# x loaded in pairs of tiles ahead of its small tables, and two products of each Strassen pair moved one pair ahead

## The chip, the cores and the metric

The kernel runs on one core of a Trainium2 chip. The time is the device time of one execution in microseconds (us); lower is better. The core has TensorE (PE, matmuls, writing to PSUM banks), VectorE (DVE), ScalarE (ACT), GpSimd (POOL) and SyncE (SP). Each engine works through its own instructions in order. Here SP issues nearly all loads, and POOL those that add onto what is already in SBUF.

## The reference

A trunk of two layers over a sequence of 512 tokens of width 1024, all in float32.

```
x: (1, 512, 1024)
layer 0:  h = rmsnorm(x);  z = h @ w_in
          a = gelu(u) * spatial_gating(gelu(v))          # 4 groups, 128 x 128 position mixing
          b = latent attention(q rank 384, kv rank 256, 32 rotary columns, 8 heads)
          x = x + concat(a, b) @ w_out
          x = x + swiglu(rmsnorm(x))                      # width 2816
layer 1:  x = x + retention(rmsnorm(x))                   # 4 heads, gated
          x = x + swiglu(rmsnorm(x))
swiglu(h) = (silu(h @ w_gate) * (h @ w_up)) @ w_down
```

## The kernel before

Activations lie transposed: x is eight tiles of 128 features by 512 tokens. Every product in full precision is made of three matmuls on halves of the numbers (`hi`, and `lo`, the rest), so each weight chunk of up to 128 x 1024 is loaded to `w_raw`, cast by ACT to `w_hi` (L214) and subtracted by DVE to `w_lo` (L215).

The weights come in one order, the tape. `tape_spec` lists the chunks, `Tape.load` makes the next one, `tape.ahead()` keeps four chunks made ahead of use (four buffers of `w_hi` and `w_lo`). `w_raw` has three buffers in the mixers and seven in the FFNs. All chunk loads go to SP's queue (L211).

**Head (L427 to L457).** x tile 0 is issued on SP, then the first chunk in four pieces, then x tiles 1 to 7. Each x tile is scaled by a gain (`scaled_parts`: `h_hi` on ACT, L356, and `h_lo` on DVE, L357), and its squares are summed for the norm (ACT L309, DVE L310). Five small tables (2 to 128 KB, 354 KB with a broadcast one of 96 KB) are issued on POOL's queue: `cgain`, `wk`, `qkg`, `rope0`, `vgain`. The first PE work is five projections of 24 matmuls with these chunks; then come the rotary key (`wk`, whose tile is scaled on DVE in L490), the attention and the gating.

**FFN (`ffn`).** Gate and up for 22 tiles of 128 columns. The first two column tiles ("whole") are done plainly. The others are done in ten pairs p = 1 to 10 by a Strassen-like scheme: seven products a pair, called A11, A12, A22 (weights as loaded, or "load"), S1, S3 (two weight blocks summed by an accumulating POOL load, L213, "sum") and S2, S4 (a block added to an earlier raw chunk by DVE, L199, "add": S2 is made from the raw chunks of A11 and S1, S4 from those of A12 and S2, so these `w_raw` buffers are held until then). A product is 24 matmuls of 256 columns (L865). It uses sums of activations, `t_hi` and `t_lo`, that ACT and DVE make at the start of the FFN (`sums`, L835 to L847, L281, L282).

PSUM banks: `xs` (`ps_x`) holds A11, onto which S2, S3 and A22 are added in turn; `vs` (`ps_v`) holds S1 and then S4; `ws` (`ps_w`) holds A12. Between these, ACT copies what is needed from `xs` to the wide tiles `rows` (`take`, L894) and DVE adds the others (`add`, L897); the next product into `xs` must wait for that copy. `finish` (L877 to L883) makes the activated result of a tile, and after the pairs 3, 7 and 10 the down projection runs over what is done so far (`down`).

The order of the products is written by hand in `ffn_steps`, for the tape and for the compute loop alike. The program is then laid out by a planner that walks it by priority in program order with its own estimates of durations, and may put a later instruction ahead of one that it takes to be not ready.

Of the kernel before, what the change touches and what calls it, by code (L numbers as in the profile page):

```python
# [10 lines left out]
F32 = mybir.dt.float32  # L11
# [5 lines left out]
P = 128  # L17
D = 1024
S = 512
KD = D // P  # L20
# [12 lines left out]
PAIRS = MF // 2  # L33
# [5 lines left out]
def ffn_steps():  # L39


    steps = [("whole", 0)]
    for p0, p1 in FF_PARTS:
        for p in range(max(p0, 1), p1):
            if p == 1:
                steps.append(("A11", p))
            steps += [("S1", p), ("S2", p), ("A12", p), ("S3", p)]
            if p + 1 < PAIRS:
                steps.append(("A11", p + 1))
            steps += [("A22", p), ("S4", p)]  # L50
        steps.append(("down", (p0, p1)))
    return steps

# [101 lines left out]
def turns(m, d):  # L155


    if m.shape[1] == 2 * d:
        return m.rearrange("p (j d) -> p d j", j=2)
    return m.rearrange("p (b j d) -> p b d j", j=2, d=d)  # L160
# [75 lines left out]
def trunk_kernel(ctx: ExitStack, tc: tile.TileContext, a: dict, out: bass.AP):  # L236
    nc = tc.nc
    const = ctx.enter_context(tc.tile_pool(name="const", bufs=1))
    parts = ctx.enter_context(tc.tile_pool(name="parts", bufs=Tape.DEPTH))
    res = ctx.enter_context(tc.tile_pool(name="res", bufs=1))  # L240
# [12 lines left out]
    def bank(name="bank"):  # L253
        return ps.tile([P, S], F32, name=name, tag="bank")

    tape = Tape(nc, parts, a["wtape"])
# [3 lines left out]

    gains = const.tile([P, 4, KD], F32, name="gains")
    nc.scalar.dma_start(out=gains, in_=a["gains"])
    x = [res.tile([P, S], F32, name=f"x{k}") for k in range(KD)]
    ident = const.tile([P, P], F32, name="ident")
    make_identity(nc, ident)
    ones = const.tile([P, P], F32, name="ones")
# [10 lines left out]
    def f32(t):  # L277
        return t.bitcast(F32)
# [66 lines left out]
    def h_tiles(k):  # L345
        return (
            hres.tile([P, S], F32R, name=f"h_hi{k}"),
            hres.tile([P, S], F32R, name=f"h_lo{k}"),
        )

    def scaled_parts(which, k):


        hi, lo = h_tiles(k)
        g = gains[:, which, k : k + 1]
        nc.scalar.activation(hi, x[k], AF.Identity, scale=g)  # L356
        nc.vector.scalar_tensor_tensor(  # L357
            lo, x[k], g, f32(hi), op0=ALU.mult, op1=ALU.subtract
        )
        return hi, lo  # L360

    def project(h, n=1, name="ps_mm", d=HALF):

        w = [tape.next() for _ in range(n)]
        accs = [bank(name) for _ in range(n)]
        nk = w[0][0].shape[1]
        for k in range(nk):
            for (hi, lo), acc in zip(w, accs):
                mm3(acc, (hi[:, k, :], lo[:, k, :]), h[k], k == 0, k == nk - 1, d)
        tape.ahead()  # L370
        return accs[0] if n == 1 else accs
# [55 lines left out]
    with ExitStack() as e:  # L427
        new_raw(e, 3)
        h = []
        for k in range(KD):  # L430
            nc.sync.dma_start(out=x[k], in_=a["xT"][k * P : (k + 1) * P, :])
            if k == 0:
                tape.load(pieces=4)
            h.append(scaled_parts(0, k))
        tape.load(pieces=2)
        tape.ahead()
        new_tmp(e)
# [5 lines left out]
        for k in range(KD):  # L443
            ss.add(x[k])

        vgain = ev.tile([P, 4], F32, name="vgain")
        cgain = ev.tile([P, 5], F32, name="cgain")
        qkg = ev.tile([P, 2, QK0], F32, name="qkg")
        rope0 = ea.tile([P, NT, 2, ROPE], F32, name="rope0")
        nc.gpsimd.dma_start(out=cgain, in_=a["lat_gT"])  # L450
        wk = ea.tile([P, KD, ROPE], F32, name="wk")
        nc.gpsimd.dma_start(out=wk, in_=a["kpe_w"])
        nc.gpsimd.dma_start(
            out=qkg, in_=a["qk_g"].rearrange("(o j) f -> o j f", o=1).broadcast_to([P, 2, QK0])
        )
        nc.gpsimd.dma_start(out=rope0, in_=a["rope0"])
        nc.gpsimd.dma_start(out=vgain, in_=a["gm_gT"])  # L457


        lat, latp = [], []  # L460
# [151 lines left out]
        w = [tape.next() for _ in range(3)]  # L612
# [37 lines left out]
        def u_tile():  # L650
# [13 lines left out]
            out=bs, in_=a["gm_b"].rearrange("(o g) t -> o g t", o=1).broadcast_to([P, 4, P])  # L664
# [147 lines left out]
    def ffn(h, ss, which):  # L812
# [7 lines left out]
        with ExitStack() as e:  # L820
# [7 lines left out]
            def wide():  # L828
                return fp2.tile([P, 2 * S], F32, name="J", bufs=4)
# [26 lines left out]
            def products(acc, name, start):  # L856

                hi, lo = tape.next()
                for k in range(KD // 2):
                    mh, ml = (turns(v, q // 2) for v in stands[name][k])  # L860
                    for f in range(2):
                        o = acc[:, f * q : (f + 1) * q]
                        cols = slice(f * P, (f + 1) * P)
                        for n, (s, m) in enumerate(((hi, mh), (hi, ml), (lo, mh))):
                            nc.tensor.matmul(  # L865
                                o,
                                s[:, k, cols],
                                m,
                                start=start and k + f + n == 0,
                                stop=k == KD // 2 - 1 and n == 2,  # L870
                                skip_group_check=True,
                            )

            def finish(m, g, u, own):

                t = fp2.tile([P, S], F32, name="t")
                nc.vector.tensor_tensor(own(t), g, own(R), op=ALU.mult)  # L877
                nc.scalar.activation(t, t, AF.Silu)
                nc.vector.tensor_tensor(own(t), own(t), u, op=ALU.mult)  # L879
                hi = fp.tile([P, S], F32R, name=f"a_hi{m % 8}")  # L880
                lo = fp.tile([P, S], F32R, name=f"a_lo{m % 8}")
                split(hi, lo, t)
                act[m] = (hi, lo)  # L883

            def in_psum(acc):
                return acc.rearrange("p (f d j) -> p f j d", f=2, j=2)

            def side(t, i):

                t = t.rearrange("p (f t) -> p f t", f=2)[:, :, i * q : (i + 1) * q]  # L890
                return t.rearrange("p f (j d) -> p f j d", j=2)

            def take(t, i, acc, sign=1.0):
                nc.scalar.activation(side(t, i), in_psum(acc), AF.Identity, scale=sign)  # L894

            def add(t, i, acc, op=ALU.add):
                nc.vector.tensor_tensor(side(t, i), side(t, i), in_psum(acc), op=op)  # L897
# [29 lines left out]
            whole = [project(h, 2)]  # L927
# [6 lines left out]
            own = lambda t: t  # L934
            for name, p in ffn_steps():
                if name == "A11":
                    xs, rows = bank("ps_x"), [wide(), None]
                    products(xs, name, True)
                    take(rows[0], 0, xs)
                    following = (xs, rows)  # L940
                    if p == 1:
                        R = ss.rows(norm)
                        for m in range(2):
                            finish(m, undone(whole[m][0]), undone(whole[m][1]), plain)
                if name == "S1":
                    xs, rows = following
                    vs = bank("ps_v")
                    products(vs, name, True)
                if name == "S2":
                    products(xs, name, False)  # L950
                    take(rows[0], 1, xs)
                if name == "A12":
                    ws = bank("ps_w")
                    products(ws, name, True)
                    add(rows[0], 0, ws)
                if name == "S3":
                    products(xs, name, False)
                    rows[1] = wide()
                    take(rows[1], 1, xs, -1.0)
                    add(rows[1], 1, vs, ALU.subtract)  # L960
                    here = (xs, rows)
                if name == "A22":
                    xs, rows = here
                    products(xs, name, False)
                    take(rows[1], 0, xs, -1.0)
                    finish(2 * p + 1, rows[1][:, :S], rows[1][:, S:], own)
                if name == "S4":
                    products(vs, name, False)
                    add(rows[0], 1, vs)
                    finish(2 * p, rows[0][:, :S], rows[0][:, S:], own)  # L970
                if name == "down":
                    last = p[1] == PAIRS
                    for m in down(*p):
                        if last:
                            yield m
                elif name != "whole":
                    tape.ahead()

    h = [scaled_parts(2, k) for k in range(KD)]
# [6 lines left out]
    h, ss = h2, ss2  # L986


    with ExitStack() as e:
# [9 lines left out]
        def parts_tile(name, n=S):  # L999
            return (od.tile([P, n], F32R, name=name + "_hi"), od.tile([P, n], F32R, name=name + "_lo"))  # L1000
# [20 lines left out]
        for hd in range(RH):  # L1021
# [17 lines left out]
            k = rotated("k", accs2)  # L1039
# [21 lines left out]
            for j in range(NT - 1):  # L1061
                n = S - j * P
# [15 lines left out]
                p = parts_tile(f"att{j}", n)  # L1078
# [117 lines left out]
```

## Time and profile before

| | |
|---|---|
| median of 3 runs | 1240.56 us (1240.27 to 1242.06) |
| profiled execution | 1239.42 us, its span 1237.6 us |
| mean granted TensorE clock | 0.997 |
| PE busy | 1219.7 us, 99% of the span |
| DVE busy | 853.4 us, 69% |
| ACT busy | 563.0 us, 45% |
| DMA | 155.32 MB, mean 125 GB/s |

The span runs from the first to the last instruction. PE's matmuls are pipelined and their ends are modelled, so its busy share says that it hardly waits, not that it is at its peak. Other engines' idle time costs nothing unless PE waits for them.

### The profile page before, as it was taken

The page shows a single profiled execution, that of the slowest core. Times are in us where ns is not written, and L with a number is a line of the kernel's source. Part 1 is how long each engine was busy: PE and PEld are TensorE (multiplying, and loading weights), DVE is VectorE, ACT ScalarE, POOL GpSimd, SP SyncE. Part 2 cuts the span into 40 slices and gives each one's busy share as a digit, 9 for nine tenths or more (in the row PEclk, how much of TensorE's full clock was granted, in tenths as well). Part 3 has the DMA queues.
Part 4 walks back from the last instruction along what each step waited for, and adds up shares of the span by engine and source line. Part 5 has one row for each costly group of instructions (what it writes and reads, how often), then busy time and mean ns, then how long its engine had stood idle before and what let it go on. Part 6 is the DMA issues. An engine that isn't in the chain of part 4 may idle for free. (4 is left out here: it accounts for less than half of the span.)

```text
span 1237.6 us, 18425 instructions
## 1 busy us (share of the span) xinstructions
PE 1219.7 (99%) x7464; PEld 1106.2 (89%) x7464; DVE 853.4 (69%) x1226; ACT 563.0 (45%) x811; POOL 85.5 (7%) x89
## 2 busy tenths in 40 slices
PE   8999999999999999999999999999998999999998
PEld 6897778898999899888888888888888989998997
DVE  6597748986597577955474574574778756875774
ACT  5465746653366245534242242242466524652551
POOL 2062000100000000000000000000010000000000
PEclk9999999999999999999999999999999999999999
DMA  7223115655575556132231332332265565754631
GB/s 233 83 75 120 35 34 171 168 173 153 139 193 172 144 144 177 72 119 102 69 102 68 103 102 69 102 103 68 86 180 161 171 151 139 204 162 128 166 108 68
DMA packets 44980, 155.32 MB, mean 125 GB/s; under 512 B 5232, under 2 KB 5776, under 8 KB 44768
## 3 DMA queue, kind: packets, MB, share of 16 engines
q1 hardware_dynamic: 38304, 130.70, 31.7%
q0 software_dynamic: 6448, 23.45, 10.7%
q8 instruction: 58, 0.95, 0.3%
q14 instruction: 26, 0.21, 0.0%
q10 hardware_dynamic: 144, 0.02, 0.0%
HBM read 152.04 MB, written 2.10 MB: 125 GB/s over the span
## 5 line engine op out<-in xcount | busy, mean ns | idle before, releaser
L214 ACT CAST w_hi<-w_raw 128x1024 fp32r<-128x1024 f32 (+3 forms) x290 | 294.3, 1021 | 479.9 <-PE ps_mm L288 230.2
L215 DVE TENSOR_TENSOR w_lo<-w_raw,w_hi 128x1024 fp32r<-128x1024 f32 (+3 forms) x290 | 345.3, 1198 | 128.2 <-ACT w_hi L214 127.7
L287 PE MATMUL ps_mm<-h_hi,w_hi 128*128 128x512 f32 x456 | 175.4, 385 | 3.7 <-ACT h_hi L356 3.5
L288 PE MATMUL ps_mm<-h_lo,w_hi 128*128 128x512 f32 x456 | 173.9, 382 | 0.7 <-DVE h_lo L357 0.6
L289 PE MATMUL ps_mm<-h_hi,w_lo 128*128 128x512 f32 x456 | 173.5, 381 | 0.0
L865 PE MATMUL ps_x<-t_hi,w_hi 128*128 128x256 f32 x480 | 133.6, 278 | 6.7 <-ACT J L894 6.6
L287 PE MATMUL ps_mm<-a_hi,w_hi 128*128 128x512 f32 x352 | 133.5, 380 | 0.3 <-ACT a_hi L281 0.3
L289 PE MATMUL ps_mm<-a_hi,w_lo 128*128 128x512 f32 x352 | 133.6, 379 | 0.0
L288 PE MATMUL ps_mm<-a_lo,w_hi 128*128 128x512 f32 x352 | 133.6, 379 | 0.0
L865 PE MATMUL ps_x<-t_lo,w_hi 128*128 128x256 f32 x480 | 132.8, 277 | 0.0
L865 PE MATMUL ps_x<-t_hi,w_lo 128*128 128x256 f32 x480 | 132.8, 277 | 0.0
L287 PEld LDWEIGHTS ps_mm<-h_hi,w_hi 128*128 128x128 f32 x456 | 86.7, 190 | 16.5 <-ACT h_hi L356 3.8
L865 PEld LDWEIGHTS ps_x<-t_hi,w_hi 128*128 128x128 f32 x480 | 92.9, 194 | 8.2 <-ACT J L894 8.2
L288 PEld LDWEIGHTS ps_mm<-h_lo,w_hi 128*128 128x128 f32 x456 | 86.6, 190 | 14.2 <-DVE h_lo L357 2.4
L289 PEld LDWEIGHTS ps_mm<-h_hi,w_lo 128*128 128x128 f32 x456 | 86.6, 190 | 12.3 <-DVE w_lo L215 0.5
L865 PEld LDWEIGHTS ps_x<-t_lo,w_hi 128*128 128x128 f32 x480 | 92.9, 194 | 0.0
L865 PEld LDWEIGHTS ps_x<-t_hi,w_lo 128*128 128x128 f32 x480 | 92.9, 193 | 0.0
L213 POOL DMA_DIRECT2D w_raw<-in_wtape x40 | 34.7, 869 | 629.4 <-DMA w_raw<-in_wtape 249.2
L287 PEld LDWEIGHTS ps_mm<-a_hi,w_hi 128*128 128x128 f32 x352 | 66.5, 189 | 10.2 <-ACT a_hi L281 1.1
L289 PEld LDWEIGHTS ps_mm<-a_hi,w_lo 128*128 128x128 f32 x352 | 66.6, 189 | 9.3
L288 PEld LDWEIGHTS ps_mm<-a_lo,w_hi 128*128 128x128 f32 x352 | 66.7, 189 | 9.1
L923 DVE TENSOR_TENSOR t<-ps_mm,R 128x512 f32<-128x512 f32 x48 | 33.1, 689 | 59.3 <-PE ps_mm L289 59.2
(226 smaller groups left out, 2595.6 us busy)
## 6 DMA issues: line engine op xcount, KB each, us to landing
w_raw<-in_wtape SPq DMA_DIRECT2D x225, 512.0 KB, 3.5
w_raw<-in_wtape POOLq DMA_DIRECT2D x40, 512.0 KB, 5.8
w_raw<-in_wtape SPq DMA_DIRECT2D x19, 384.0 KB, 3.2
x<-in_xT SPq DMA_DIRECT2D x8, 256.0 KB, 6.4
out_T<-x SPq DMA_DIRECT2D x8, 256.0 KB, 2.0
decay<-in_decay POOLq DMA_DIRECT2D x1, 1024.0 KB, 7.2
w_raw<-in_wtape SPq DMA_DIRECT2D x4, 128.0 KB, 4.4
w_raw<-in_wtape SPq DMA_DIRECT2D x2, 256.0 KB, 6.2
```

The source lines that it names most:

```text
L213: nc.gpsimd.dma_start(out=t[:, c], in_=more[:, c], accum_op=ALU.add)
L214: nc.scalar.copy(hi[:, c], t[:, c])
L215: nc.vector.tensor_tensor(lo[:, c], t[:, c], hi[:, c].bitcast(F32), op=ALU.subtract)
L287: nc.tensor.matmul(acc, sh, mh, start=start, stop=False)
L288: nc.tensor.matmul(acc, sh, ml, start=False, stop=False)
L289: nc.tensor.matmul(acc, sl, mh, start=False, stop=stop)
L865: nc.tensor.matmul(o, s[:, k, cols], m, start=start and k + f + n == 0, stop=k == KD // 2 - 1 and n == 2, skip_group_check=True,)
L923: nc.vector.tensor_tensor(plain(t), undone(accs[j]), plain(R), op=ALU.mult)
```

## The change

x becomes one tile of eight parts, and the array in memory is laid out so that a partition's row of several x tiles is contiguous. x tile 0 is issued first, then the first weight chunk in two pieces, then x tile 1, then tiles 2 and 3, 4 and 5, 6 and 7 as one load each. The five small tables go to SP's queue at the place in the program where they were issued on POOL's, which is behind the first four weight chunks.

In the FFN, A11 and A12 of pair 1 come before S1 of pair 1; later in each pair, A11 of the next pair stands between S2 and S3, and A12 of the next pair between S3 and A22. The products, their operands and the engines that do each step stay the same.

```diff
 def ffn_steps():
-    steps = [("whole", 0)]
+    steps = [("whole", 0), ("A11", 1), ("A12", 1)]
     for p0, p1 in FF_PARTS:
         for p in range(max(p0, 1), p1):
-            if p == 1:
-                steps.append(("A11", p))
-            steps += [("S1", p), ("S2", p), ("A12", p), ("S3", p)]
-            if p + 1 < PAIRS:
-                steps.append(("A11", p + 1))
-            steps += [("A22", p), ("S4", p)]
+            following = [(n, p + 1) for n in ("A11", "A12") if p + 1 < PAIRS]
+            steps += [("S1", p), ("S2", p), *following[:1], ("S3", p)]
+            steps += [*following[1:], ("A22", p), ("S4", p)]
         steps.append(("down", (p0, p1)))
...
-    x = [res.tile([P, S], F32, name=f"x{k}") for k in range(KD)]
+    x_all = res.tile([P, KD, S], F32, name="x")
+    x = [x_all[:, k, :] for k in range(KD)]
...
-        for k in range(KD):
-            nc.sync.dma_start(out=x[k], in_=a["xT"][k * P : (k + 1) * P, :])
-            if k == 0:
-                tape.load(pieces=4)
-            h.append(scaled_parts(0, k))
+        for k0, k1 in ((0, 1), (1, 2), (2, 4), (4, 6), (6, 8)):
+            nc.sync.dma_start(out=x_all[:, k0:k1, :], in_=a["xP"][:, k0:k1, :])
+            if k0 == 0:
+                tape.load(pieces=2)
+            for k in range(k0, k1):
+                h.append(scaled_parts(0, k))
         tape.load(pieces=2)
         tape.ahead()
...
-        nc.gpsimd.dma_start(out=cgain, in_=a["lat_gT"])
+        nc.sync.dma_start(out=cgain, in_=a["lat_gT"])
         wk = ea.tile([P, KD, ROPE], F32, name="wk")
-        nc.gpsimd.dma_start(out=wk, in_=a["kpe_w"])
-        nc.gpsimd.dma_start(
+        nc.sync.dma_start(out=wk, in_=a["kpe_w"])
+        nc.sync.dma_start(
             out=qkg, in_=a["qk_g"].rearrange("(o j) f -> o j f", o=1).broadcast_to([P, 2, QK0])
         )
-        nc.gpsimd.dma_start(out=rope0, in_=a["rope0"])
-        nc.gpsimd.dma_start(out=vgain, in_=a["gm_gT"])
+        nc.sync.dma_start(out=rope0, in_=a["rope0"])
+        nc.sync.dma_start(out=vgain, in_=a["gm_gT"])
...
                 if name == "A11":
-                    xs, rows = bank("ps_x"), [wide(), None]
-                    products(xs, name, True)
-                    take(rows[0], 0, xs)
-                    following = (xs, rows)
+                    following = (bank("ps_x"), [wide(), None])
+                    products(following[0], name, True)
+                    take(following[1][0], 0, following[0])
...
                 if name == "A12":
                     ws = bank("ps_w")
                     products(ws, name, True)
-                    add(rows[0], 0, ws)
+                    add(following[1][0], 0, ws)
...
-        "xT": np.ascontiguousarray(w["x"][0].T),
+        "xP": w["x"][0].T.reshape(KD, P, S).transpose(1, 0, 2),
```

## Rows read from the trace of the kernel before

**Rows 1.** The page, totals: busy us (share of the span) x instructions.
```profile
PE 1219.7 (99%) x7464; PEld 1106.2 (89%) x7464; DVE 853.4 (69%) x1226; ACT 563.0 (45%) x811; POOL 85.5 (7%) x89
```

**Rows 2.** Groups by line, PE, 5 to 28: busy, mean ns | idle before, releaser.
```profile
L287 PE MATMUL ps_mm<-h_hi,w_hi 128*128 128x512 f32 x25 | 10.1, 411 | 3.5 <-ACT h_hi L356 3.5
L288 PE MATMUL ps_mm<-h_lo,w_hi 128*128 128x512 f32 x24 | 9.9, 417 | 0.6 <-DVE h_lo L357 0.6
```

**Rows 3.** Windows: stretch, length, each engine's busy time, granted clock, DMA share, GB/s.
```profile
5.00:9.50 4.50, 1.10 (x7) 0.65 (x5) 1.75 (x5) 2.09 (x6) 0.00 (x0) 1.00 0.99 315
9.50:14.20 4.70, 4.00 (x9) 2.60 (x10) 4.66 (x7) 4.70 (x10) 4.20 (x6) 0.64 1.05 391
...
931.20:943.00 11.80, 8.98 (x65) 8.79 (x66) 11.41 (x14) 6.07 (x9) 0.87 (x1) 0.86 0.57 143
943.00:962.00 19.00, 19.00 (x172) 19.00 (x172) 14.70 (x18) 11.43 (x15) 1.72 (x2) 1.00 0.70 185
```

**Rows 4.** Groups by line, PE, 921 to 945 (pair 1, second FFN).
```profile
L865 PE MATMUL ps_x<-t_hi,w_hi 128*128 128x256 f32 x16 | 5.4, 336 | 4.0 <-ACT J L894 4.0
...
L865 PE MATMUL ps_v<-t_lo,w_hi 128*128 128x256 f32 x8 | 2.4, 301 | 0.7 <-DVE t_lo L282 0.7
```

**Rows 5.** Groups by line, PE, 218 to 252 (first FFN).
```profile
L865 PE MATMUL ps_x<-t_hi,w_hi 128*128 128x256 f32 x34 | 9.6, 281 | 2.5 <-ACT J L894 2.5
```

**Rows 6.** Timeline of ACT, 911 to 935: start, us, instruction [idle before <-releaser].
```profile
921.54 1.04 ACT L214 CAST w_hi<-w_raw 128x1024 fp32r<-128x1024 f32 x1 [6.46 <-DMA w_raw<-in_wtape]
...
930.61 0.58 ACT L894 ACTIVATE J<-ps_x 128x512 f32<-128x512 f32 x1
```

**Rows 7.** DMA issues, 912.5 to 913: KB each, median us to landing.
```profile
w_raw<-in_wtape POOLq DMA_DIRECT2D x1, 512.0 KB, 8.7
```

**Rows 8.** Timeline of SP's queue, 0 to 20.
```profile
0.74 0.38 SPq L431 DMA_DIRECT2D x<-in_xT  x1
...
3.06 4.33 SPq L431 DMA_DIRECT2D x<-in_xT  x7
```

**Rows 9.** DMA issues, 0.7 to 1.2, 2.5 to 3.5 and 6.9 to 7.3.
```profile
x<-in_xT SPq DMA_DIRECT2D x1, 256.0 KB, 2.8
...
x<-in_xT SPq DMA_DIRECT2D x1, 256.0 KB, 5.7
...
x<-in_xT SPq DMA_DIRECT2D x1, 256.0 KB, 6.3
```

**Rows 10.** Timeline of DVE, 0 to 42: tiles 1 and 7.
```profile
9.54 0.75 DVE L357 SCALAR_TENSOR_TENSOR h_lo<-x,gains,h_hi 128x512 fp32r<-128x512 f32 x1 [1.33 <-ACT h_hi L356]
...
16.11 0.74 DVE L357 SCALAR_TENSOR_TENSOR h_lo<-x,gains,h_hi 128x512 fp32r<-128x512 f32 x1
```

**Rows 11.** Timeline of ACT, 0 to 42: the second piece of the first chunk.
```profile
5.80 0.41 ACT L214 CAST w_hi<-w_raw 128x256 fp32r<-128x256 f32 x1 [0.53 <-DMA w_raw<-in_wtape]
```

**Rows 12.** The chain that ended last: start, us, what.
```profile
1200.02 2.69 PE ps_v L865 x24
```

**Rows 13.** Timeline of PE, 922.3 to 922.6 and 1195.3 to 1197.4.
```profile
922.41 0.38 PE L288 MATMUL ps_mm<-h_lo,w_hi 128*128 128x512 f32 x1
...
1195.55 0.38 PE L287 MATMUL ps_mm<-a_hi,w_hi 128*128 128x512 f32 x1
...
1197.07 0.38 PE L865 MATMUL ps_x<-t_hi,w_hi 128*128 128x256 f32 x1
```

**Rows 14.** Timeline of ACT, 1185 to 1210.
```profile
1195.68 0.83 ACT L214 CAST w_hi<-w_raw 128x768 fp32r<-128x768 f32 x1 [1.85 <-PE ps_x L865]
1196.42 0.59 ACT L894 ACTIVATE J<-ps_x 128x512 f32<-128x512 f32 x1
```

**Rows 15.** Timeline of SP's queue, 244.5 to 246.5.
```profile
245.04 0.33 SPq L211 DMA_DIRECT2D w_raw<-in_wtape  x1
```

**Rows 16.** Timeline of ACT, 261 to 265.
```profile
262.37 1.05 ACT L214 CAST w_hi<-w_raw 128x1024 fp32r<-128x1024 f32 x1 [1.09 <-PE ps_v L865]
```

**Rows 17.** DMA issues, 248.5 to 249.5.
```profile
w_raw<-in_wtape POOLq DMA_DIRECT2D x1, 512.0 KB, 6.7
```

More of the change, by code (lines that the diff above doesn't have):

```diff
@@ L960, in ffn @@
                     add(rows[1], 1, vs, ALU.subtract)
-                    here = (xs, rows)
                 if name == "A22":
-                    xs, rows = here
                     products(xs, name, False)
```

## The prediction

> **What bounds the kernel now.** I read the page's totals first: TensorE (PE) is busy 1219.7 us of the span's 1237.6 [rows 1], so only a change that takes PE's idle or slow time can pay. The program's matmuls are the same before and after, so the change can only move waits. Then I asked each stretch for PE's idle time and what released it, and for its granted clock. The reader is to see two kinds of place.
>
> The first is the head. After its first three real matmuls PE waits 3.5 us for `h_hi` of x tile 1 and 0.6 us for `h_lo` tiles [rows 2], and from 9.5 to 14.2 the granted clock is 0.64, a mix of the 2.4 and the 1.2 GHz level, after that idle [rows 3].
>
> The second is the first Strassen pair (p = 1) of each FFN. In the second FFN PE waits 4.0 us, in two waits, for ACT's `take` (L894) and 0.7 us for `t_lo` [rows 4]; then the granted clock is 0.86 over 11.8 us, so (1 - 0.86) x 11.8 = 1.65 us more are lost. After that PE is busy 19.00 of 19.00 us [rows 3]: the pairs that follow have nothing to win. In the first FFN the same two waits make 2.5 us [rows 5].
>
> What makes `take` late in the second FFN is ACT's order [rows 6]. ACT waits 6.46 us for the DMA of S1's summed weights before it casts them at 921.54; the second half of the activation sums, the next casts and the takes stand behind that cast, the first take at 930.61. DVE, which needs ACT's output, idles with it and then has everything to do at once. The summed chunk is late because its accumulating POOL transfer takes 8.7 us to land [rows 7].
>
> **The change part by part: the head.** x tile 0 is issued at 0.74 [rows 8] and lands after 2.8 us, at 3.5; tile 1 is issued only at 3.06, behind four weight pieces, and lands after 5.7, at 8.8; tile 7, issued at about 7.0, lands after 6.3, at 13.3 [rows 9]. So tiles 2 to 7 come (13.3 - 8.8)/6 = 0.75 us apart. The change sends, after tile 0, two pieces of 256 KB instead of four of 128 KB, then tile 1, then three pairs of tiles, with no table among them. At 0.75 us per 256 KB tile 1 lands at 3.5 + 3 x 0.75 = 5.8 and tile 7 at 3.5 + 9 x 0.75 = 10.3, both 3.0 us sooner. The longer packets by themselves I put at nothing, since this takes the rate of the old ones; what they add to the rate, DVE hides.
>
> For behind the data the next limit is DVE. From tile 1's `h_lo` at 9.54 to the end of tile 7's at 16.85 it works with hardly a break, seven `h_lo` and three sums [rows 10]. The same chain from 9.54 - 3.0 = 6.5 ends at 13.9: the head gains 3.0 us. If the sums (some 0.7 us each) came after the `h_lo`, the data would be the bound, 10.3 + 0.75 (ACT) + 0.75 = 11.8, a gain of 5.1. On the other side the first weight piece is twice as long, 0.4 us more on ACT ahead of tile 1 (a 256-column cast is 0.41 [rows 11]) and as much on DVE, and DVE's L490 needs `wk`, now queued behind the fourth weight chunk: I allow 1.0 us for all, a gain of 2.0. I take 3.0, since the sums lay in between before too.
>
> The five tables go from POOL's queue to SP's, behind the fourth chunk, which waits for one of three `w_raw` buffers. PE needs none of them before the products that follow the five latent projections; SP pays five issues of about 0.4 us (as tile 0's, [rows 8]) ahead of chunk 5, whose issue waits for a buffer anyhow. That cover makes it nothing; without it, 2 us of SP.
>
> The Trainium skill (DMA: Bandwidth & Descriptors, "Issuing engines are not separate DMA queues") says that transfers of all issuing engines run on the same 16 engines and interleave, so another queue frees no bandwidth. By it only the tables' later place helps, and their 354 KB would be worth about 0.8 us at the page's 436 GB/s (an estimate from that page). In the rows tile 1 takes 2.9 us longer to land than tile 0 with tables and weight pieces among them, and the sum goes by the rows.
>
> **The pairs.** Old order of a pair: S1 S2 A12 S3 A11' A22 S4 (' marks the next pair). New: S1 S2 A11' S3 A12' A22 S4, with A11 and A12 of pair 1 ahead of its S1. A product is 24 matmuls, 2.7 us [rows 12]. In pair 1 the products between A11's take and S2 are now A12 and S1, not S1 alone, so S2 has 2.7 us more of cover and S1 reads `t_lo` 2.7 us later: the first take wait and the `t_lo` wait go. Before S3 there are five products instead of four.
>
> For S3's wait there are two bounds. If ACT's second take ends at the same moment as before, S3 starts then too, with one product more done: 2.7 us won in the second FFN. If ACT is no longer blocked, all the waits go, and with them the slow clock: 4.0 + 0.7 + 1.65 = 6.4. I lean to the second: with four `w_hi` buffers A12's chunk now takes the one that was free for S1's, and S1's cast needs one that the "whole" products hold until 922.8 [rows 13], later than its data came (921.5). A planner that sees that buffer taken puts the activation sums ahead of the cast, into the time in which ACT and DVE sat idle. I take 6.0, bounds 2.7 and 6.4. In the first FFN the whole is 2.5 and the first wait alone about half; I take 2.3, bounds 1.3 and 2.5.
>
> **What it costs: the last pair.** Pair 10 has no next pair, so its new order is S1 S2 S3 A22 S4: A12, which stood between S2 and S3, is gone from there. S3 adds into the bank that ACT must first take. The nearest row is the same adjacency that exists already, S3 before A22: `ps_x` ends by 1195.55 and A22 starts at 1197.07, 1.5 us later, most of it filled by matmuls of the down projection [rows 13]. ACT's take lay behind a cast of 0.83 us and took 0.59 itself [rows 14]. Between S2 and S3 nothing can fill: the down chunk's buffer is freed by S2 itself. With the cast ahead it is 1.5 us, without about 0.6. I take 1.0 in each FFN, together -2.0 (bounds -1.2, -3.0).
>
> **What it costs: buffers.** Counted in steps of the tape, A11's `w_raw` buffer is held 11 steps instead of 9 and A12's 9 instead of 4, so of seven on average three instead of two are not free for loads. A summed chunk, S3 of pair 3, was issued at 245.04 [rows 15] and cast at 262.37 [rows 16], a lead of 17.3 us; its POOL part is issued about 249 and lands in 6.7 [rows 17], at 255.6. So 6.8 us are to spare. One buffer of five less takes a fifth of the lead, 3.5 us; it stays hidden with about 3 to spare. Cost nothing; uncovered it is a rival, below.
>
> **Sum.** 3.0 + 2.3 + 6.0 - 2.0 = 9.3 us. The profiled execution took 1239.4 us around its span of 1237.6, which gives 1230.1. It lies 1.1 us under the median shown, 1240.56, from which the same sum gives 1231.3. I say 1231.2. Bounds: 2.0 + 1.3 + 2.7 - 3.0 = 3.0 and 5.1 + 2.5 + 6.4 - 1.2 = 12.8 us, so 1237.6 and 1227.8.
>
> **Rivals.** (a) The wait moves: ACT still casts S1 first and blocks, and S3 waits as long as before. The idle in [rows 6] speaks for it, the buffer argument against. The second FFN then gives 2.7, the sum is 6.0, the time 1234.6. (b) The head gives nothing because DVE, not the data, sets it: DVE is busy 4.66 of 4.70 us from 9.5 to 14.2; against it, only 1.75 of 4.50 before [rows 3]. Then 6.3 us, 1234.3. (c) The other side: seven `w_raw` buffers don't do. If the summed chunks came later than their casts, ACT, in order, would hold the takes behind it in all 20 pairs. The sign turns at 9.3/20 = 0.5 us of PE wait a pair; at 1 us it is 1240.56 - 9.3 + 20 = 1251.3. It needs leads shorter by 7 us; I count 3.5. (d) The change doesn't do what it says in the head: if x as one tile were tracked as a whole, each of the four loads after tile 0 would wait for the readers of the one before, some 2.8 + 0.7 + 0.7 = 4.2 us, and tile 7 would land at 3.5 + 4 x 4.2 = 20.3, 7.0 later than now; with the FFNs' 6.3 that is 1241.3. Against it: `w_raw` is one tile too, and ACT casts its pieces one by one as they land [rows 11].
>
> **Chances.** Forecast 0.59 (its own range 1227.8 to 1233.5); (a) 0.20; (b) 0.09; (c) 0.06; (d) 0.06. About 0.2%, 2.5 us, is what a measurement can tell from no change. Faster, below 1238.1, are the forecast, (a) and (b), less 0.02 for the sum of all lower bounds: 0.86. Same 0.07, slower 0.07, from (c), (d) and that rest. The range 1227 to 1238 holds the forecast, (a), (b) and both sums of bounds.
>
> **What the profile after would show.** Right: `h_hi` of tile 1 starts near 6 and no half clock follows 9.5; in pair 1 of each FFN `ps_w` comes before the first `ps_v`, ACT's wait for the DMA ahead of S1's cast is gone or late, and PE's waits for L894 are under 1 us; a new PE gap of about 1 us before S3 of pair 10, twice. Wrong: ACT waits for DMA before casts in every pair, or DVE waits for `wk`.

## The result and the profile after

The change made the kernel slower: 1283.46 us (median of 6 runs, 1279.91 to 1285.4) against 1240.38 (6 runs, 1239.8 to 1242.06), a ratio of 1.0344 [1.0329, 1.0358]. The prediction said 1231.2 us, so its sign was wrong. The profiled execution's span is 1281.5 us, 43.9 more than before.

The page of the changed kernel, totals and two of its costliest groups (group; busy us, mean ns; idle before and what ended most of it):

```profile
PE 1234.3 (96%) x7464; PEld 1117.4 (87%) x7464; DVE 851.8 (66%) x1224; ACT 561.8 (44%) x809; POOL 83.7 (7%) x84
...
L864 PE MATMUL ps_x<-t_hi,w_hi 128*128 128x256 f32 x480 | 139.3, 290 | 28.3 <-ACT J L893 28.2
...
L196 DVE TENSOR_TENSOR w_raw<-w_raw 128x1024 f32<-128x1024 f32 x40 | 48.8, 1221 | 79.7 <-DMA w_raw<-in_wtape 79.5
```

No engine has more work than in [rows 1]: DVE and ACT are busy a little less, with the same instructions. PE is "busy" 14.6 us longer with as many matmuls, the mark of a lower clock (the mean granted clock is 0.986, where it was 0.997), and its share falls from 99% to 96%, the mark of waits. Two groups name the waits: products of the pairs behind ACT's `take` (L893), and DVE's additions of raw weights (L196, which make the chunks S2 and S4) behind DMAs. The views of waits for the two kernels tell how much of that is new (waited for; us in total, times, longest). Before, DVE, PE and ACT:

```profile
DVE w_raw L199 <- DMA w_raw<-in_wtape: 18.3, 4, 4.9
...
PE ps_x L865 <- ACT J L894: 6.6, 4, 2.8
...
ACT a_hi L281 <- DVE t L879: 34.7, 37, 1.4
```

After:

```profile
DVE w_raw L196 <- DMA w_raw<-in_wtape: 79.5, 16, 6.8
...
PE ps_x L864 <- ACT J L893: 28.2, 10, 5.5
...
ACT a_hi L279 <- DVE t L878: 59.8, 25, 7.1
```

All three grew, and they are links of one chain. It is read best in pair 2 of the first FFN, where PE's longest gap lies. PE ends A11' of pair 3 and waits for the take of S2's product:

```profile
255.46 0.28 PE L864 MATMUL ps_x<-h_hi,w_lo 128*128 128x256 f32 x1
261.19 0.58 PE L864 MATMUL ps_x<-t_hi,w_hi 128*128 128x256 f32 x1 [5.46 <-ACT J L893]
```

ACT (start, us, instruction, idle before and releaser) had the take, at 260.54, behind two casts of `a_hi` and the work between them. The first of these casts waited 6.48 us for a product on DVE:

```profile
257.08 0.62 ACT L279 CAST a_hi<-t 128x512 fp32r<-128x512 f32 x1 [6.48 <-DVE t L878]
257.60 1.04 ACT L211 CAST w_hi<-w_raw 128x1024 fp32r<-128x1024 f32 x1
258.55 0.62 ACT L877 ACTIVATE t<-t 128x512 f32<-128x512 f32 x1
260.02 0.62 ACT L279 CAST a_hi<-t 128x512 fp32r<-128x512 f32 x1 [0.84 <-DVE t L878]
260.54 0.59 ACT L893 ACTIVATE J<-ps_x 128x512 f32<-128x512 f32 x1
```

DVE, in turn, stood 6.77 us in front of an addition, with that product (L878) and the low part of S3's weights (L212) queued behind it:

```profile
255.22 1.23 DVE L196 TENSOR_TENSOR w_raw<-w_raw 128x1024 f32<-128x1024 f32 x1 [6.77 <-DMA w_raw<-in_wtape]
256.36 0.68 DVE L878 TENSOR_TENSOR t<-t,J 128x512 f32<-128x512 f32 x1
256.96 0.69 DVE L876 TENSOR_TENSOR t<-J,R 128x512 f32<-128x512 f32 x1
257.56 1.22 DVE L212 TENSOR_TENSOR w_lo<-w_raw,w_hi 128x1024 fp32r<-128x1024 f32 x1
```

What it waited for is the accumulating half of S1's chunk of pair 3, issued on POOL at 249.67 and landed at 255.12 (POOL's row, and the transfer with its KB and us from issue to landing):

```profile
249.67 0.85 POOL L210 DMA_DIRECT2D w_raw<-in_wtape  x1 [7.43 <-DMA w_raw<-in_wtape]
...
w_raw<-in_wtape POOLq DMA_DIRECT2D x1, 512.0 KB, 5.5
```

The point to see is the next pair of times in the trace: S1's chunk is cast only at 266.29, 11.2 us after it landed, and the chunk that this addition makes, S2 of pair 3, at 268.96:

```profile
266.29 1.05 ACT L211 CAST w_hi<-w_raw 128x1024 fp32r<-128x1024 f32 x1 [2.77 <-issue]
...
268.96 1.05 ACT L211 CAST w_hi<-w_raw 128x1024 fp32r<-128x1024 f32 x1 [1.14 <-issue]
```

So no weights of pair 3 were late for their product. The addition was merely placed 13.7 us ahead of its own cast in DVE's order, behind a transfer in flight, and DVE takes its instructions in that order. Over the pairs of the first FFN an S2 addition starts a median of 14.0 us before its cast (7.8 to 19.1); before the change it was 5.2 (4.7 to 21.2). The Trainium skill (PSUM — Partial Sum Buffer, "Engine vs sequencer instructions") says that the queues of ScalarE, VectorE and GpSimdE are strictly first in, first out. The rows agree: L878 read nothing of that transfer and started 0.1 us before the addition's listed end.

PE's gaps follow from these waits in size. In pairs 2, 5, 6 and 9 of both FFNs PE stands in front of S3 after DVE has stood in front of the next pair's S2 addition, and in seven of these eight places PE's gap is DVE's wait less 1.15 or 1.16 us (6.77 and 5.62 in the place shown; in the eighth, 5.65 and 4.80). But a wait of DVE need not reach PE. In pairs 4 and 8 of both FFNs the additions wait 6.3 to 6.7 us, no shorter, and PE has no gap, since it is at the down projection then. The four waits of the kernel before stand at these same places.

Behind the gap comes a second loss. Windows of that place (length, busy PE, PEld, DVE, ACT, POOL, granted clock, DMA share, GB/s):

```profile
255.00:261.50 6.50, 1.04 (x8) 0.85 (x7) 6.28 (x8) 3.58 (x6) 0.00 (x0) 0.81 0.22 78
261.50:266.00 4.50, 4.50 (x23) 4.50 (x23) 3.63 (x4) 2.02 (x3) 0.86 (x1) 0.52 0.40 61
266.00:276.00 10.00, 10.00 (x92) 10.00 (x92) 6.93 (x9) 5.86 (x8) 0.00 (x0) 1.00 0.69 238
```

After 5.6 us of idleness (from start to start of the matmuls, less the usual 0.11; the 5.46 of the row counts from a modelled end) PE runs 4.5 us at a granted clock of 0.52, nearly all of it at 1.2 GHz, which costs (1 - 0.52) x 4.5 = 2.2 us more: the gap of 5.6 costs 7.8. Gaps of over 0.3 us in the two FFNs, counted in the same way here and below, add up to 40.6 us, in pairs 1, 2, 5, 6, 9 and 10 of both; the pitch of the products exceeds their median by 54.6 us in all, where it was 9.7 before, and the rest is mostly half clock.

All runs, with marks read from their traces: the start of the key product `ps_kpe`, the length of each FFN from its first to its last product in `ps_x`, `ps_v` or `ps_w`, and DVE's waits in front of additions. Spans need the first FFN's later start and what follows it as well.

```
                              median us  key   FFN 1   FFN 2   adds' waits
before                          1240.4   38.9  275.7   279.6   18.3 (4)
after                           1283.5   37.6  301.7   299.6   79.5 (16)
e1  new head only               1237.3   38.0  275.5   279.6   19.4 (4)
e2  new pairs only              1288.5   39.2  304.7   303.2   88.7 (18)
e3  after + late adds           1236.7   37.6  277.3   278.1   none
e4  after + eight buffers       1261.5   37.2  291.2   293.2   51.4 (14)
e5  e3 + last pair's S1 moved   1231.4   37.6  276.1   272.4   none
e6  before, six buffers         1237.7   40.1  275.2   280.0   28.9 (5)
e7  before + late adds          1237.2   39.2  275.2   277.1   none
e8  e1 + four first pieces      1238.3   38.1  275.5   279.7   18.8 (4)
e9  before + tables on SP       1236.9   37.5  275.9   279.6   20.4 (4)
e10 e5 with the old head        1233.1   39.5  275.3   272.5   none
e11 e5 with eight buffers       1228.2   37.4  272.4   272.4   none
e12 after + late S2 adds        1230.0   37.5  274.0   274.0   none
```

### The profile page after: what moved, and what is told of

Read it like the earlier page. It is cut to its first block, busy times and chain, and to the rows that moved or that the text cites. A ratio compares the mean times of both kernels' runs of the same rounds, so it can differ in the third digit from the quotient of the medians.

```text
span 1281.5 us, 18377 instructions
## 1 busy us (share of the span) xinstructions
PE 1234.3 (96%) x7464; PEld 1117.4 (87%) x7464; DVE 851.8 (66%) x1224; ACT 561.8 (44%) x809; POOL 83.7 (7%) x84
## 5 line engine op out<-in xcount | busy, mean ns | idle before, releaser
L211 ACT CAST w_hi<-w_raw 128x1024 fp32r<-128x1024 f32 (+2 forms) x288 | 292.9, 1027 | 492.9 <-PE ps_mm L286 230.5
L212 DVE TENSOR_TENSOR w_lo<-w_raw,w_hi 128x1024 fp32r<-128x1024 f32 (+2 forms) x288 | 343.6, 1204 | 122.0 <-ACT w_hi L211 121.2
L864 PE MATMUL ps_x<-t_hi,w_hi 128*128 128x256 f32 x480 | 139.3, 290 | 28.3 <-ACT J L893 28.2
L864 PE MATMUL ps_x<-t_hi,w_lo 128*128 128x256 f32 x480 | 138.0, 287 | 3.6 <-DVE w_lo L212 3.6
L864 PE MATMUL ps_x<-t_lo,w_hi 128*128 128x256 f32 x480 | 137.8, 287 | 0.0
L864 PEld LDWEIGHTS ps_x<-t_hi,w_hi 128*128 128x128 f32 x480 | 97.6, 203 | 31.4 <-ACT J L893 31.4
L196 DVE TENSOR_TENSOR w_raw<-w_raw 128x1024 f32<-128x1024 f32 x40 | 48.8, 1221 | 79.7 <-DMA w_raw<-in_wtape 79.5
L864 PEld LDWEIGHTS ps_x<-t_hi,w_lo 128*128 128x128 f32 x480 | 97.9, 204 | 3.8 <-DVE w_lo L212 3.8
L864 PEld LDWEIGHTS ps_x<-t_lo,w_hi 128*128 128x128 f32 x480 | 97.7, 203 | 0.0
```

The lines of the kernel that those rows point to most:

```text
L196: nc.vector.tensor_tensor(t[:, :w], t[:, :w], self.raws[how[2]][:, :w], op=ALU.add)
L211: nc.scalar.copy(hi[:, c], t[:, c])
L212: nc.vector.tensor_tensor(lo[:, c], t[:, c], hi[:, c].bitcast(F32), op=ALU.subtract)
L864: nc.tensor.matmul(o, s[:, k, cols], m, start=start and k + f + n == 0, stop=k == KD // 2 - 1 and n == 2, skip_group_check=True,)
```

## The experiments: which half, and which engine

**e1: the new head with the old pairs.** The loads and tables of the change, the old list of steps and the old loop body.

> Only the head of the change, the pairs in their old order. From the traces of before and after: the rotary key's products start 1.3 us sooner in the changed kernel (37.6 for 38.9), and all that follows up to the first FFN keeps these 1.3 us. Every theory of the loss in the FFNs expects 1239.1, ratio 0.999. The prediction's 3.0 us for the head would be 1237.4.

Measured 1237.33 us (10 runs, 1235.88 to 1239.08), 0.9977 [0.9967, 0.9986] of the kernel before. By these medians the head is worth 2.9 us, which is the prediction's figure and not the 1.3 us read from the traces; the FFNs are as they were.

**e2: the old head with the new pairs.**

> Only the new order of the pairs, the head of before. If the loss has nothing to do with the head, 1283.5 + 1.3 = 1284.8, ratio 1.036. If the head's shift had helped to cause it, clearly less.

Measured 1288.54 us (4 runs), 1.0388 [1.0364, 1.0413], 3.7 us above the 1284.8 expected, with both FFNs 3.0 and 3.6 us longer than in the whole change. The whole loss is in the moved chunks.

**e3: the whole change, each addition queued on DVE behind the low part of the chunk before it.** Data, transfers and buffers are asked for in the order of the change; only DVE's order differs, and with it the moment at which an addition frees a buffer.

```diff
-            nc.vector.tensor_tensor(t[:, :w], t[:, :w], self.raws[how[2]][:, :w], op=ALU.add)
+            with self.tc.issue_after(self.last_lo):
+                nc.vector.tensor_tensor(t[:, :w], t[:, :w], self.raws[how[2]][:, :w], op=ALU.add)
...
-            nc.vector.tensor_tensor(
+            self.last_lo = nc.vector.tensor_tensor(
...
-            )
+            ).ins
```

> The whole change, and each add of raw chunks (S2, S4) is queued on DVE behind the w_lo subtraction of the chunk before it. Theory 1 (DVE stands in order before an add that was put there too early, and everything behind it is late): DVE's 79.5 us of waits for DMA before the add go, PE's waits in the pairs go, and the time is that of the prediction with the measured head, 1240.4 - 1.3 - 8 + 2 = 1233. Theory 2 (the summed chunks come too late for the products themselves): the wait moves to ACT's cast of S1 or S3, and the time stays above 1270. Theory 3 (the new order of PSUM use and of take on ACT makes the waits): no change, 1283.

Measured 1236.65 us (10 runs), 0.9972 [0.9957, 0.9986]: the change's time falls by 46.8 us by the order alone; the 1233 of the theory is missed by 3.7 us, which e5 and e12 take up. DVE waits in front of no addition, PE's waits for takes fall to 6.2 us, and pair 1 of both FFNs has no gap. That refutes the readings by which the weights came too late for the products, or by which the accumulators or the takes were tied by the new order of products itself.

**e4: the whole change with eight buffers of raw weights.** The warm-up's ones tile is half as wide and its products twice as many, to make room.

```diff
-            new_raw(e, 7)
+            new_raw(e, 8)
```

> The whole change with eight w_raw buffers in the FFNs instead of seven; to make room the warm-up matmuls use a 64-column tile, twice as many. Theory 1 and theory 2: each load can be issued about one release sooner, some 3 to 4 us, against DVE waits of 2.5 to 6.8 us before the add: most of the loss goes, 1235 to 1250. Theory 3: buffers don't matter, 1283.

Measured 1261.5 us (4 runs, 1258.56 to 1266.03), 1.0164 [1.0146, 1.0182]. Earlier transfers shorten the additions' waits to 51.4 us and halve the loss, as they should if the buffers work through the additions' waits; the 1235 to 1250 us expected was missed, since these waits did not go.

**e6: the kernel before with six buffers in place of seven.**

> The kernel before, unchanged but for six buffers of raw weights in the FFN in place of seven. Theory (the lead of S1's raw chunk over the add that reads it is what the change used up, and DVE stands in order behind that add): the chunks are asked for one turn later, about 3.5 us, DVE's wait in front of the adds grows from 18 us in all to some 50 us, and part of it reaches PE through the takes: 1250 us (1244 to 1265). Rival (the lead is not what matters, only the new order of the chunks is): DVE's waits grow but PE does not notice, 1240 to 1242 us.

Measured 1237.68 us (10 runs, 1236.0 to 1240.64), 0.9982 [0.9973, 0.9991]. My theory, as put there, was wrong: the additions wait 28.9 us in place of 18.3, not 50, and PE does not notice, as the rival had it. But 28.0 of the 28.9 us fall in pairs 4 and 8, where the additions of this order stand 18 to 19 us ahead of their casts and PE is at the down projection. Elsewhere they stand 4 to 10 us ahead and wait 0.9 us at most. So a wait of 7 us is harmless where nothing behind it is due soon, and of the pairs that lose in the changed kernel this run says little. That the time even fell by 2.4 us, below the rival's range, is not explained: the profiled execution of this kernel was its slowest run (1240.64), and its marks show no gain. Gains of 2 to 3 us in other kernels here are to be read beside this one.

**e12: the whole change, late additions for S2 alone.** S2's addition reads S1's chunk, which is in flight; S4's reads chunks that have long been in.

```diff
-            with self.tc.issue_after(self.last_lo):
+            with self.tc.issue_after(self.last_lo) if key[2] == "S2" else ExitStack():
```

> The whole change with the late add for the S2 chunks alone; the adds of S4 stay where the planner puts them (21 to 24 us ahead of their own cast, in the middle of the list). An S2 add reads the raw chunk of S1, which is still in flight; an S4 add reads two chunks that have long been in. Theory (the loss is DVE standing in front of an operand in flight, and everything queued behind it): nearly as fast as with all adds late, 1236 to 1240 us, and DVE waits nowhere in front of an add for a DMA. Rival (it is enough that adds of 1.2 us stand ahead of work that is due sooner, in flight or not): half of the loss stays, 1250 to 1262 us.

Measured 1229.95 us (4 runs, 1229.7 to 1230.04), 0.992 [0.9903, 0.9936]. The theory held, but its 1236 to 1240 us was too slow: this is 6.7 us faster than e3. The group of the additions in its trace:

```profile
L198 DVE TENSOR_TENSOR w_raw<-w_raw 128x1024 f32<-128x1024 f32 x40 | 48.8, 1220 | 0.2
```

and PE's first group of the pairs, whose 28.3 us of idleness were the sign of the loss:

```profile
L866 PE MATMUL ps_x<-t_hi,w_hi 128*128 128x256 f32 x480 | 132.3, 276 | 0.1
```

So the S4 additions, whose operands are in, do no harm here by standing early (11.6 us ahead of their casts in e12, by the median). The S2 additions of 1.2 us, in front of an operand in flight, were the whole loss.

## The experiments: the last pair, the controls, the head

**e5: e3, and in the last pair S1's product between S2 and S3.** `products` takes weights that were fetched before as one more argument.

```diff
...
-                    vs = bank("ps_v")
-                    products(vs, name, True)
+                    vs, w1 = bank("ps_v"), None
+                    if p == PAIRS - 1:
+                        w1 = tape.next()
+                    else:
+                        products(vs, name, True)
                 if name == "S2":
                     products(xs, name, False)
                     take(rows[0], 1, xs)
+                    if w1:
+                        products(vs, "S1", True, w1)
```

> The whole change with the late add, and in the last pair of each FFN the product S1 computed between S2 and S3 instead of before S2. In the run with the late add alone PE stands 2.26 and 2.41 us ahead of S3 in the last pairs and then runs for some microseconds at a granted clock near 0.86. Theory (the take of S2's product has no product to hide behind there): both gaps vanish and the half clock behind them too, 5 to 6 us less than the late add alone, 1231 us (1229.5 to 1233). Rival (the take is late because ACT stands on the cast of S4's chunk, and would hold PE wherever the product lies): the gap moves behind S1's product at nearly its length less 2.7 us, or DVE's work for A22 comes late instead: 1234 to 1237 us.

Measured 1231.35 us (5 runs, 1230.49 to 1233.57), 0.9935 [0.9922, 0.9947], the time that the theory gave. But its account of e3's gaps (2.26 and 2.41 us) was only half of it, as the trace of e3 shows. ACT there, in the last pair:

```profile
481.52 1.04 ACT L213 CAST w_hi<-w_raw 128x1024 fp32r<-128x1024 f32 x1 [0.59 <-DVE w_raw L198]
482.47 0.59 ACT L895 ACTIVATE J<-ps_x 128x512 f32<-128x512 f32 x1
```

and DVE:

```profile
480.19 1.22 DVE L198 TENSOR_TENSOR w_raw<-w_raw 128x1024 f32<-128x1024 f32 x1
```

The take stands behind the cast of S4's chunk, and that cast waits for S4's addition, which e3 had made late. Where it is not made late, the gap is half as long. In e12 PE (S2's last product, then S3 behind two products of the down projection):

```profile
479.79 0.28 PE L866 MATMUL ps_x<-t_hi,w_lo 128*128 128x256 f32 x1
480.92 0.48 PE L287 MATMUL ps_mm<-a_hi,w_hi 128*128 128x512 f32 x1 [0.85 <-ACT w_hi L213]
481.24 0.38 PE L288 MATMUL ps_mm<-a_lo,w_hi 128*128 128x512 f32 x1
481.45 0.34 PE L866 MATMUL ps_x<-t_hi,w_hi 128*128 128x256 f32 x1
```

ACT there has the take behind the cast of the down projection's chunk:

```profile
480.03 0.83 ACT L213 CAST w_hi<-w_raw 128x768 fp32r<-128x768 f32 x1 [0.43 <-PE ps_x L866]
480.77 0.59 ACT L895 ACTIVATE J<-ps_x 128x512 f32<-128x512 f32 x1
```

The gap is 1.02 us in both FFNs of e12, and 1.02 in both of the changed kernel too (at 507.5 and 1235.4), with no half clock behind it in e12. e5 hid in part what the late S4 additions had made.

**e7: the kernel before with late additions, a control.** The edit is that of e3.

> The kernel before with each add put on DVE behind the low part of the chunk before it, and nothing else. A control: where the adds are early enough anyway this can only take away DVE's 18 us of waiting for raw chunks. Theory: pair 1's gaps stand for another reason (takes without cover), so the time stays within 1.5 us of 1240.4. Rival (the late add by itself makes the kernel faster, and the moved chunks give nothing): 1236 to 1237 us, as the whole change with it.

Measured 1237.22 us (10 runs), 0.9979 [0.997, 0.9988]: 2.8 us faster, beyond the 1.5 that the theory allowed. The second gap of pair 1 in the second FFN falls from 2.94 to 1.69 us, no half clock follows (granted 1.00 from 931 to 943, where it was 0.86), and that FFN is 2.5 us shorter. The cause is another one than in the changed kernel: no addition of pair 1 waits for a transfer there. DVE's timeline in the kernel before:

```profile
931.42 1.23 DVE L199 TENSOR_TENSOR w_raw<-w_raw 128x1024 f32<-128x1024 f32 x1
932.57 1.22 DVE L215 TENSOR_TENSOR w_lo<-w_raw,w_hi 128x1024 fp32r<-128x1024 f32 x1
933.70 1.28 DVE L877 TENSOR_TENSOR t<-ps_mm,R 128x512 f32<-128x512 f32 x2
```

and in e7:

```profile
928.96 3.49 DVE L217 TENSOR_TENSOR w_lo<-w_raw,w_hi 128x1024 fp32r<-128x1024 f32 x3
932.37 1.28 DVE L879 TENSOR_TENSOR t<-ps_mm,R 128x512 f32<-128x512 f32 x2
```

The addition of 1.2 us stood ahead of products on which ACT's take hangs; without it they start 1.3 us sooner, the take too (937.68 for 939.00). That is the rival of e12, small and in the old order: an addition can cost its own length though its operands are in. e3 and e7 together (1236.7 and 1237.2) would say that the moved chunks give nothing; e12 and e10 say otherwise.

**e10: e5 with the old head.**

> The old head with the moved chunks, the late add, and S1's product of the last pair between S2 and S3. The late add alone on the old order gave 1237.2 us, and the new head alone 1237.3. Theory (with the order of DVE and the last pair mended, the moved chunks are worth most of the 8.3 us that the pair-1 gaps and the half clock behind them were forecast at, and part of it is what the late add had given): 1232.9 us (1231.5 to 1234.5), which is the repaired whole change plus the head's 1.7. Rival (the repaired version is fast by the late add and the head, and the moved chunks give nothing of their own): 1236 to 1237.5 us.

Measured 1233.06 us (5 runs, 1232.83 to 1234.52), 0.9949 [0.9936, 0.9963], as the theory had it. The moved chunks with the mended order are worth 6.8 us without the head, 4.2 of them beyond what late additions give the old order.

**e11: e5 with eight buffers.**

> The repaired whole change (late add, last pair) with eight buffers of raw weights in place of seven, and the warm-up products on a ones tile of half the width, twice as many, to make room. With the early adds the eighth buffer was worth 22 us. Theory (the buffers did harm only through the adds that DVE met too early): with the late add the chunks are early enough with seven, and the eighth gives under 1.5 us, 1230 to 1231.5 us. Rival (the moved chunks really leave too little lead, and ACT's 37 us of waits for raw chunks cost PE): 1227 to 1229 us.

Measured 1228.18 us (4 runs, 1227.59 to 1228.66), 0.9907 [0.9893, 0.992], the fastest of all, and at the rival's end. All of it is in the first FFN (276.1 to 272.4 us), where e5 has gaps of 1.21 us at 268 and 1.39 and 0.86 at 484 to 486, and e11 has none. e12 has none at 268 either, with seven buffers. So it is likely that the late S4 additions, which hold two raw buffers longer, made the shortage that the eighth buffer ends (ACT waits 36.8 us for raw chunks in e5 and 8.7 in e12); e12 with eight buffers was not tried.

**e8: e1 with the first weight chunk in four pieces.**

> The kernel before with the new head alone (pairs of x tiles, tables on SP), but with the first weight chunk in four pieces as before the change, not two. With two pieces the first product began at 6.20 us where it had begun at 5.13, and the head gave 1.3 us at the key product where 3.0 were forecast. Theory (the larger first piece costs the missing part): the first product begins at 5.1 to 5.3 us, and the whole is 0.5 to 1.1 us below the new head with two pieces, 1236.5 us (1235.8 to 1237). Rival (PE waits for the x tiles and for what is made of them in any case, so that an earlier start only lengthens a later wait): 1237.3 us, and up to 0.5 us more, as the two more issues on SP make the x tiles later.

Measured 1238.27 us (11 runs), 0.9984 [0.9975, 0.9993], no better than e1. The first product begins at 6.20 us all the same. With four pieces it begins at 5.13 in the profile before, 5.18 in e2, 5.85 in e10 and 6.20 in e6, e7 and e9, so that this start varies with the execution. The rival was right, 0.5 us beyond its range.

**e9: the kernel before with the five tables on SP, and nothing else.**

> The kernel before with the five small tables asked for on SP, behind the first weights, in place of POOL; x and its loads as before. In the traces so far the key product starts at 38.9 to 40.1 us with the old head and at 37.2 to 38.1 with the new one, 1.7 us apart where 3.0 were forecast. Theory (the tables stood ahead of the x tiles on the DMA engines, and the longer packets add little): the first gap of PE shrinks and the key product starts at 37.6 to 38.4, 1238.5 us. Rival (the layout of x brings it: half as many issues and packets of twice the length): the key product stays at 38.9 or later, 1240 to 1240.5 us.

Measured 1236.87 us (11 runs), 0.9977 [0.9968, 0.9986]: 3.0 us, as much as the whole new head by the medians. The groups of PE from 5 to 28 us that answer to [rows 2], in e9:

```profile
L287 PE MATMUL ps_mm<-h_hi,w_hi 128*128 128x512 f32 x27 | 11.3, 425 | 0.7 <-ACT h_hi L356 0.7
L288 PE MATMUL ps_mm<-h_lo,w_hi 128*128 128x512 f32 x26 | 10.7, 418 | 0.7 <-DVE h_lo L357 0.7
```

and in the changed kernel:

```profile
L285 PE MATMUL ps_mm<-h_hi,w_hi 128*128 128x512 f32 x27 | 10.7, 396 | 1.4 <-ACT h_hi L354 1.4
L286 PE MATMUL ps_mm<-h_lo,w_hi 128*128 128x512 f32 x26 | 10.3, 397 | 1.4 <-DVE h_lo L355 1.4
```

The wait of 3.5 us falls to 0.7 and to 1.4. The longer packets of x and its pairs of tiles add nothing that these runs can tell. The edit changes the queue of the tables and their place at once; no run tells the two apart.

## Why the prediction was wrong, point by point

**The step that failed is "buffers: cost nothing".** It measured the lead of a summed chunk, S3, against ACT's cast of that chunk, and found 6.8 us to spare. S3 has no earlier reader. But the first to read S1's raw chunk is not its own cast; it is DVE's addition for S2, and where that stands in DVE's order was never looked up. The lead against the casts did hold in the main (11.2 us to spare for S1 of pair 3; ACT waits for raw chunks 11.4 us in all, where it waited 19.7). The lead against the addition did not, since the addition had moved from 5 to 14 us ahead of its cast. What that cost by the runs is 46.8 us (e3) to 53.5 (e12).

**Rival (c)** had the right side and the wrong place. It had the summed chunks too late for ACT's casts, with all 20 pairs losing alike and a price of 1 us a pair. What the trace shows is DVE held at an addition, ACT held by DVE's product, the take held in ACT: one link more than the rival had, in pairs 1, 2, 5, 6 and 9, with up to 5.6 us of gap and 2.2 of half clock each. Its condition, leads shorter by 7 us, was not the one that decides. The sign that it named for the wrong case, ACT waiting for DMA before casts in every pair, is not in the profile after, nor is DVE waiting for `wk`; of the signs for the right case, `h_hi` of tile 1 near 6 us (6.38) and the end of ACT's wait before S1's cast in pair 1 did come. The sign of the loss is DVE's.

**The head** came out at its number, 3.0 us forecast and 2.9 (e1) and 3.0 (e9) measured by medians, but in part by luck. The chain that was to end at 13.9 us, tile 7's `h_lo`, ends at 15.31 in the changed kernel, 1.5 us sooner than before and not 3.0:

```profile
13.90 1.41 DVE L355 SCALAR_TENSOR_TENSOR h_lo<-x,gains,h_hi 128x512 fp32r<-128x512 f32 x2
```

The key product starts at a median of 39.2 us in the five profiles with the whole old head and at 37.6 in the eight with the new one. The rest of the 3 us lies elsewhere. The mean granted clock of all runs is 0.9982 in e9 and 0.9964 in the kernel before beside it, which over 1240 us makes 2.2 us (an estimate, if PE was at work all that time); in e1 it makes 2.1. The single profiles can't place it: the half clock from 9.5 to 14.2 us [rows 3] is gone in the changed kernel (granted 1.00) and not in e9 (0.64), with key products at 37.6 and 37.5. I gave the gain to the earlier place of the x tiles and the longer first piece a price; e9 shows that the tables' move alone gives as much, and e8 no gain from the shorter piece. And e6, with the old head, fell by 2.4 us for no known reason, so 3.0 is not firm. Rivals (b) and (d), which took the head's gain away, did not come. The Trainium skill (DMA: Bandwidth & Descriptors, "Issuing engines are not separate DMA queues") says that another queue frees no bandwidth. No run here shows it, since e9 moved queue and place together. The estimate from that page, 0.8 us, is 2.2 us less than e9's gain; the sum from the rows was nearer.

**The pairs.** With S2's additions mended (e12) pair 1 has no gap in either FFN, the rival (a) did not come, and the first FFN is 275.7 - 274.0 = 1.7 us shorter, the second 279.6 - 274.0 = 5.6. Forecast were 2.3 - 1.0 = 1.3 and 6.0 - 1.0 = 5.0. The second bound of S3's wait was the right one, and the half clock behind it went with it. But not all of it is the moved chunks': late additions alone take 2.5 us off the second FFN (e7), which the forecast did not have, so the moved chunks add 277.1 - 274.0 = 3.1 there.

**The last pair**: 1.0 us forecast in each FFN, 1.02 measured, and that is half luck. 1.0 was a middle between 1.5 us with a cast ahead of the take and 0.6 without. The cast was ahead, and S3 starts 1.66 us after S2's last matmul; but two matmuls of the down projection stand in between, where the prediction said that nothing could.

So the sum without its failed step came out near: 1231.2 forecast, 1229.95 measured once the additions of S2 stood where their operand is in. Part of this is luck, since the mended order gives the old kernel something too: e12 lies 7.3 us under e7, and 9.3 were forecast. The kernel before with late S2 additions alone was not run.

**What stays open.** Why the order in which the program lists DVE's work puts S2's additions so much earlier once A11' and A12' are a pair ahead is not shown: the trace holds the order, not the estimate behind it. It would fit that the addition's other operand, A11's chunk, is now in long before. The 2.4 us of e6 are not explained, and where the runs of one kernel differ in granted clock is not known beyond the profiled ones.

## What to carry to other kernels

When chunks or loads are moved ahead, list every reader of each transfer, and for each the engine and what stands behind it in that engine's order; the lead that counts is that of the first reader, and the buffers' lead against the last consumer can be long while an early reader stalls its whole engine. A small instruction on a side engine that waits for a transfer in flight is priced by what is queued behind it and how soon that is due: here 20 additions of 1.2 us, placed too early, cost 53.5 us, and four of their longest waits cost nothing, as PE was at the down projection. Before a change that loses is thrown away, mend the one order that broke: the same change was 0.8% faster than the kernel before with one instruction a pair kept back (e12).

## What the runs showed of the hardware

In the changed kernel a gap of 5.6 us on PE was followed by 4.5 us at a granted clock of 0.52, and the 4.8 us one at 986 in the second FFN by 4.0 us at 0.50; the gaps of 1.02 us in e12 by none (1.00 from 478 to 495). DVE, standing 6.77 us in front of an addition, started no later instruction in that time. The accumulating transfers of 512 KB took 5.1 to 9.7 us from issue on POOL to landing over all traces (median 5.5 on the page of the changed kernel, with the plain ones of SP at 3.4).
